# A 512-column matmul whose columns are visited in another order, in four classes of products of a hybrid decoder layer

## The chip, the cores and the metric

The kernel is written in a tile language for Trainium2 and runs on one core of one chip. The metric is device time in microseconds (us), from the launch of the program to its end. One core has five engines that run side by side: TensorE (PE in the profile, with its weight loads shown apart as PEld), VectorE (DVE), ScalarE (ACT), GpSimd (POOL) and SyncE (SP, which issues DMAs here). Each executes its own instructions in program order and waits on semaphores for the others.

## The reference

One layer of a hybrid decoder on x of shape (1, 1024, 1024): a normalised and modulated input projection, two head groups side by side (a gated linear recurrence and a chunked gated delta rule), an output projection with a residual, and a squared-ReLU MLP of width 4096. Cut to what the change touches:

```python
h = rms_norm(x, norm_mix_w[l]) * (1.0 + sc1) + sh1
proj = h @ w_in[l]
...
mix = jnp.concatenate([out_lru, out_gdn], axis=-1) @ w_out[l]
x = x + g1 * mix

h = rms_norm(x, norm_mlp_w[l]) * (1.0 + sc2) + sh2
x = x + g2 * (jnp.square(jax.nn.relu(h @ w_up[l])) @ w_down[l])

return rms_norm(x, final_norm_w)
```

## The kernel before

Every large product is made from fp32 values that have been split in two parts of fewer bits, a high part h and a low part l, in a 4-byte type (fp32r) of which the array takes one column at a time. A product is then three matmuls, h·h, h·l and l·h, all added in one PSUM tile: that is `mm3` (line 648). Its arguments are the PSUM tile p, the pair w (the stationary operand, loaded into the array) and the pair a (the moving operand, whose columns stream through the array). A matmul of the stages below has a stationary operand of 128x128 and a moving operand of 128x512, that is 512 columns of 4 bytes in each partition; its result fills a whole PSUM tile of 128x512 fp32. Column number n of the moving operand gives column number n of the result.

The stages on TensorE in order of time, with the tile names of the profile:

- the input projection (`k_p`, `z_p`, `q_p`, `v_p`, `lx_p`, `ly_p`; moving operands of 342 columns for most), with the delta rule and the recurrence worked between its products, up to 410 us;
- the output projection, `gemm_o` (line 1494), in two halves: first the delta-rule heads (`wg`), then the recurrence's (`wl`). Each half makes 8 x 2 result tiles of 4 k-steps x 3 matmuls, so 192 matmuls of 512 columns. After each `wl` row block, `norm2` (line 1523) normalises and transposes it (`h2T`);
- the MLP's first product, `up` (line 1657), from 512 to 826 us. It uses a Strassen-like scheme: for each of 16 weight blocks n, seven products numbered `at` = 1 to 7 by operand sums. `product` (line 1632) makes one, 4 k-steps x 3 matmuls = 12 matmuls of 512 columns. Number 2 is the only one that writes the PSUM tile `upy` (16 x 12 = 192 matmuls), numbers 5 and 3 write `upz` (384, half of them of number 3), numbers 1, 6, 7 and 4 write `upx` (768);
- the MLP's second product, `products` (line 1808, tile `dn`), from 826 to 1138 us, by the same scheme.

Operations are recorded first, with an estimated duration each (`length`, line 504), and then ordered by a list scheduler, which emits them from one line, so that nearly all instructions have L462 in the profile. The order of the instructions on every engine is thus set by the estimates. For a matmul of this type the estimate was taken from the size of the last dimension of the moving operand.

One other place is spoken of later: the forward substitution in `inverse` (line 1141), 31 steps on VectorE over a tile `xx` of 32 rows of 32 fp32 in each partition. Step j reads and writes n = 31 - j rows, the first m = j + 1 columns of each, so that it goes m columns in a run and then to the next row, 128 bytes further. Its products stand in `ftmp`, packed:

```python
for j in range(31):
    n, m = 31 - j, j + 1
    t3 = tmp[:, :n * m].rearrange("p (i c) -> p i c", c=m)
    V.tensor_tensor(out=t3, in0=gg[:, j + 1:, j:j + 1].to_broadcast([P, n, m]),
                    in1=xx[:, j:j + 1, 0:m].to_broadcast([P, n, m]), op=ALU.mult)
    V.tensor_tensor(out=xx[:, j + 1:, 0:m], in0=xx[:, j + 1:, 0:m], in1=t3, op=ALU.subtract)
```

Of the kernel before, what the change touches and what calls it, by code (L numbers as in the profile page):

```python
# [468 lines left out]
def free_size(ap):  # L469
    n = 1  # L470
    for d in ap.shape[1:]:
        n *= d
    return n


class Proxy:
# [27 lines left out]
    def length(self, name, out, ins, k):  # L504
        n = max([free_size(out)] + [free_size(v) for v in ins[:1]])
        ptr = sum(free_size(v) == 1 for v in ins[1:]) if n > 1 else 0
        psum = any(isinstance(v, View) and v.buf.tag == "ps" for v in ins)
        if self.eng == "PE":
            if name == "transpose":
                return 0.108  # L510
            if ins[1].dtype == F32R:
                return (max(ins[1].shape[-1], 64) / 2267.0 + 0.006) * (0.5 if ins[1].shape[0] == 64 else 1.0)
            return 4 * max(ins[1].shape[-1], free_size(ins[0])) / 2420.0 if ins[1].shape[-1] > 1 else 0.13
        if self.eng == "DVE":
            fast = name in ("tensor_scalar", "tensor_copy", "memset") and not psum
            if name == "tensor_tensor_scan":
                return 0.15 + n / 480.0
            if name == "transpose":
                return 0.05 + n / 550.0
            return (0.145 if psum else 0.155) + n / (1920.0 if fast else 960.0) + 0.06 * ptr  # L520
        if self.eng == "ACT":
            return (0.16 if psum else 0.195) + n / 1200.0 + 0.1 * max(ptr, "accum_out" in k)
        if k.get("op") == ALU.pow:
            return 0.4 + 0.156 * n
        if name == "memset":
            return 0.1 + n / 1200.0
        if name == "tensor_scalar":
            return 0.15 + n / 720.0
        if name == "scalar_tensor_tensor":
            return 0.15 + n / 380.0  # L530
        return 0.13 + n / 448.0
# [45 lines left out]
def hybrid_body(ctx, tc, x, c, norm_mix_w, norm_mlp_w, w_mod, b_mod, w_in,  # L577
# [41 lines left out]
    def ps(name):  # L619
        return buf(pp, "ps", N_PS, [P, 512], F32, name)  # L620
# [14 lines left out]
    def mm(o, lhsT, rhs, start=True, stop=True, **kw):  # L635
        PE.matmul(o, lhsT, rhs, start=start, stop=stop, **kw)
# [8 lines left out]
        rec.add("PE", several, (), {}, [x[0] for x in items], [y for x in items for y in x[1:3]], dur)  # L645
        rec.ops[-1].work = share * dur

    def mm3(p, w, a, start, stop, **kw):
        mm(p, w[0], a[0], start, False, **kw)
        mm(p, w[0], a[1], False, False, **kw)  # L650
        mm(p, w[1], a[0], False, stop, **kw)
# [167 lines left out]
    class Proj:  # L819
# [11 lines left out]
        def third(self, i):  # L831
            self.p[i] = p = ps(f"{self.name}_p{i}")
            s, _ = third(i)
            for k in range(NK):
                ks = slice(k * P, (k + 1) * P)
                mm3(p[:, 0:342], (self.w[0][:, ks], self.w[1][:, ks]), (hT[k][0][:, s], hT[k][1][:, s]),
                    k == 0, k == NK - 1)
            if i == 2:
                self.o = 3 if self.staged else 0
                self.dst = big(f"{self.name}_st", F32, T + self.o)  # L840
                if self.staged:
                    V.memset(self.dst[:, 0:3], 0.0)
                self.b = small(f"{self.name}_b", 1)
                V.tensor_copy(self.b, p[:, 340:341])
            if self.b is not None:
                for e in list(self.p):
                    _, d = third(e)
                    A.activation(self.dst[:, self.o + d.start:self.o + d.stop], self.p.pop(e)[:, 0:d.stop - d.start],
                                 AF.Identity, bias=self.b)

    class Key(Proj):
        def part(self, p, o, ks, c0, c1, start=True):
            for k in ks:
                kc = slice((k % 2) * 512 + self.h * P, (k % 2) * 512 + self.h * P + P)
                mm3(p[:, o:o + c1 - c0], (wkq[k // 2][0][:, kc], wkq[k // 2][1][:, kc]), (hT[k][0][:, c0:c1], hT[k][1][:, c0:c1]),
                    start and k == 0, k == NK - 1, skip_group_check=True)
# [147 lines left out]
    for k in range(NK):  # L1004
        a, b = (q_[:, T:T + 2] for q_ in hT[k])
# [488 lines left out]
    def gemm_o(cats, ws, t, i, name, then):  # L1494
        p = ps(name)
        s = halves[i]
        hf, tt = t // 4, t % 4
        rec.bb = True
        for k in range(4):
            ts_ = slice((k % 2) * 512 + tt * P, (k % 2) * 512 + (tt + 1) * P)  # L1500
            a, w = cats[(hf, k // 2)], ws[k]
            mm3(p, (a[0][:, ts_], a[1][:, ts_]), (w[0][:, s], w[1][:, s]), k == 0, k == 3)
        rec.bb = False
        then(p, s)

# [4 lines left out]
    for t in range(NT):  # L1510
        for i in range(2):
            gemm_o(gcat, gw_, t, i, f"wg{t}{i}",
                   lambda p, s: V.tensor_tensor(out=x1[t][:, s], in0=p, in1=x1[t][:, s], op=ALU.add))
# [68 lines left out]
    for t in range(NT):  # L1582
        for i in range(2):
            gemm_o(lcat, lw, t, i, f"wl{t}{i}",
                   lambda p, s: V.scalar_tensor_tensor(out=x1[t][:, s], in0=p, scalar=rsl[:, t:t + 1], in1=x1[t][:, s],
                                                       op0=ALU.mult, op1=ALU.add))
        if t == 0:
            dump("x1", x1[0])
        norm2(t)
# [42 lines left out]
    def product(p, at, w, start, stop):  # L1632
        rec.bb = True
        for k in range(4):
            ks, ds_ = slice(k * P, (k + 1) * P), slice((k % 2) * 512, (k % 2) * 512 + 512)
            b = opb[at][k // 2]
            mm3(p, (w[0][:, ks], w[1][:, ks]), (b[0][:, ds_], b[1][:, ds_]), start and k == 0, stop and k == 3, skip_group_check=True)
        rec.bb = False

    def relu2(dst, src_):  # L1640
# [16 lines left out]
    def up(n):  # L1657
        w = weights_up(n)
        f0, f1, ek = big(f"act{n}_0"), big(f"act{n}_1"), big(f"ek{n}")
        c11, c12, c21, c22 = f0[:, lo_], f0[:, hi_], f1[:, lo_], f1[:, hi_]  # L1660
        px, py = ps(f"upx{n}"), ps(f"upy{n}")
        product(px, 1, next(w), True, True)
        A.copy(ek[:, lo_], px)
        product(py, 2, next(w), True, True)
        V.tensor_tensor(out=c11, in0=py, in1=ek[:, lo_], op=ALU.add)
        relu2(c11, c11)
        yield
        pz = ps(f"upz{n}")
        product(px, 6, next(w), False, True)
        A.copy(ek[:, hi_], px)  # L1670
        yield
# [162 lines left out]
    for at in (1, 2, 6, 5, 7, 3, 4):  # L1834
# [18 lines left out]
        for j in range(4):  # L1853
# [10 lines left out]
            p = bank[j]  # L1864
# [49 lines left out]
```

## Time and profile before

| | |
|---|---|
| median of the runs (2) | 1149.38 us (1149.0 to 1149.75) |
| the profiled execution | 1147.2 us, of which the span of its instructions is 1145.5 us |
| TensorE busy | 1128.2 us, 98% of the span |
| VectorE, ScalarE, GpSimd busy | 833.7, 612.7, 266.0 us |
| granted TensorE clock, mean | 0.994 |
| mean DMA rate | 204 GB/s |

The page of a profile gives busy time per engine, the chain of waits that ended last, and groups of equal instructions with their count, busy time, mean duration and the idle time ahead of them. Matmuls are pipelined: a matmul of 512 columns is listed with a duration of some 395 ns, while the next one starts about 232 ns after it. What a matmul costs in a stream is therefore the step from one start to the next, which the timeline shows, and not its listed duration.

### The profile page before, as it was taken

To read this page: it belongs to the slowest core of one execution; us is meant where nothing else is said; L and a number is where in the kernel's file an instruction comes from. 1 tells how busy PE (TensorE), PEld (TensorE's weight loads), DVE (VectorE), ACT (ScalarE), POOL (GpSimd) and SP (SyncE) were. 2 spreads that over 40 slices of the span, in tenths; PEclk is the share of its full clock that TensorE was granted. 3 is DMA by queue.
4 is the path that set the end of the run, shared out by engine and by line. 5 is a ranking of instruction groups with operands and counts; after the bars stand their busy time and mean duration, and the time that the engine had idled before them with its cause. 6 is when DMAs were issued, how large, how long until landed. Compare 5 with 4: busy or idle time off the path is not lost.

```text
span 1145.5 us, 16586 instructions
## 1 busy us (share of the span) xinstructions
PE 1128.2 (98%) x6288; PEld 968.9 (85%) x6288; DVE 833.7 (73%) x1143; ACT 612.7 (53%) x961; POOL 266.0 (23%) x161
## 2 busy tenths in 40 slices
PE   8999999999999999999999999999999999999997
PEld 5889998999999987888888788887888888888886
DVE  4749998688899697879757876777775574864573
ACT  5637535445377866577554555556645433453352
POOL 1101110011112425100012231234500086823030
PEclk9999999999999999999999999999999999999999
DMA  9615834247533372331477787767999667764631
GB/s 345 215 51 205 292 111 131 92 148 235 195 114 125 105 268 94 109 135 49 156 243 247 262 277 230 246 215 253 382 392 400 238 226 272 277 231 155 220 147 74
DMA packets 126257, 233.75 MB, mean 204 GB/s; under 512 B 10785, under 2 KB 49886, under 8 KB 126178
## 3 DMA queue, kind: packets, MB, share of 16 engines
q1 hardware_dynamic: 126178, 232.71, 58.4%
q8 instruction: 49, 0.80, 0.3%
q14 instruction: 30, 0.25, 0.1%
HBM read 173.93 MB, written 58.74 MB: 203 GB/s over the span
## 4 chain that ended last, share of the span: by engine, by line
PE 85%; DVE 6%; ACT 5%; DMA 2%; issue 2%; POOL 1%; SPq 0%; POOLq 0%; ACTq 0%; DVEq 0%
PE dn L462 27%; PE upx L462 15%; PE upz L462 8%; PE k_p L462 4%; PE z_p L462 4%; PE wl L462 4%; PE upy L462 4%; PE v_p L462 4%; PE q_p L462 3%; PE ch L462 2%; PE ly_p L462 2%; PE lx_p L462 1%; ACT ta L462 1%; DVE xr L462 1%; PE cho L462 1%
## 5 line engine op out<-in xcount | busy, mean ns | idle before, releaser
L462 PE MATMUL upx<-h2h,U 128*128 128x512 f32 x512 | 168.0, 395 | 0.0
L462 PEld LDWEIGHTS upx<-h2h,U 128*128 128x128 f32 x512 | 96.0, 188 | 22.7 <-DVE U L462 0.3
L462 POOL TENSOR_TENSOR wd<-wd,wd 128x512 f32<-128x512 f32 x32 | 49.3, 1546 | 225.7 <-DMA wd<-in_w_down_dram 154.2
L462 ACT ACTIVATE act<-act 128x512 f32<-128x512 f32 x112 | 70.4, 632 | 57.0 <-DVE act L462 55.4
L462 PE MATMUL upx<-h2l,U 128*128 128x512 f32 x256 | 100.8, 394 | 0.0
L462 DVE TENSOR_TENSOR U<-wu,U 128x512 fp32r<-128x512 f32 x112 | 87.0, 795 | 18.4 <-ACT U L462 18.2
L462 PE MATMUL upz<-h2h,U 128*128 128x512 f32 x256 | 85.1, 394 | 0.0
L462 ACT CAST U<-wu 128x512 fp32r<-128x512 f32 x112 | 66.9, 618 | 32.0 <-DVE wu L462 10.4
L462 PEld LDWEIGHTS upx<-h2l,U 128*128 128x128 f32 x256 | 48.1, 188 | 11.3
L462 PEld LDWEIGHTS upz<-h2h,U 128*128 128x128 f32 x256 | 48.0, 188 | 11.3
L462 PE MATMUL upz<-h2l,U 128*128 128x512 f32 x128 | 50.5, 395 | 0.0
L462 DVE TENSOR_TENSOR act<-upz,ek 128x512 f32<-128x512 f32 x32 | 22.0, 687 | 38.9 <-PE upz L462 30.2
L462 ACT COPY ek<-upx 128x512 f32<-128x512 f32 x48 | 28.1, 585 | 37.2 <-PE upx L462 35.9
L462 PE MATMUL upy<-h2h,U 128*128 128x512 f32 x128 | 42.8, 395 | 0.2 <-DVE U L462 0.2
L462 POOL TENSOR_TENSOR xb<-xb,keep 128x512 f32<-128x512 f32 x8 | 13.5, 1697 | 117.8 <-ACT R_6h L462 82.3
L462 PE MATMUL v_p<-hl,v_wh 128*128 128x342 f32 x96 | 32.3, 337 | 2.0 <-issue 2.0
L462 DVE TENSOR_TENSOR wu<-wu,wu 128x512 f32<-128x512 f32 x48 | 33.8, 714 | 0.2
L462 PE MATMUL v_p<-hh,v_wl 128*128 128x342 f32 x96 | 32.4, 337 | 0.0
L462 PE MATMUL lx_p<-hh,lx_wh 128*128 128x342 f32 x96 | 32.2, 336 | 0.0
L462 PE MATMUL lx_p<-hl,lx_wh 128*128 128x342 f32 x96 | 32.0, 333 | 0.0
L462 PE MATMUL v_p<-hh,v_wh 128*128 128x342 f32 x96 | 31.9, 332 | 0.0
L462 PE MATMUL lx_p<-hh,lx_wl 128*128 128x342 f32 x96 | 31.7, 330 | 0.0
(587 smaller groups left out, 3580.8 us busy)
## 6 DMA issues: line engine op xcount, KB each, us to landing
L<-aod SPq DMA_DIRECT2D x56, 512.0 KB
R<-in_w_down_dram SPq DMA_DIRECT2D x40, 512.0 KB
wu<-in_w_up_dram SPq DMA_DIRECT2D x32, 512.0 KB
aod<-as SPq DMA_DIRECT2D x64, 256.0 KB
wd<-in_w_down_dram SPq DMA_DIRECT2D x32, 512.0 KB
aod<-act SPq DMA_DIRECT2D x48, 256.0 KB
sc_w<-in_w_mod_dram SPq DMA_DIRECT2D x16, 512.0 KB
x<-in_x_dram SPq DMA_DIRECT2D x16, 512.0 KB
```

What stands on the lines that cost most here:

```text
L462: op.fn(*[res(v) for v in op.a], **{n: res(v) for n, v in op.k.items()})
```

## The change

`mm3` gets an argument `walk` = (a, c). Where it is given, the moving operands and the PSUM row are both viewed as a blocks of b runs of c columns, p (a b c), and visited in the order b, a, c: c neighbouring columns from the first block, c from the second and so on through all a blocks, and then the next run of c from each. As both sides are permuted alike, column n still gives column n. With 512 columns:

| products | tile | walk (a, c) | order of columns | distance of a step to the next block |
|---|---|---|---|---|
| output projection, delta-rule half | `wg` | (2, 2) | pairs, in turn from the two halves of the row | 256 columns, 1024 bytes |
| output projection, recurrence half | `wl` | (2, 16) | runs of 16, in turn from the two halves | 256 columns, 1024 bytes |
| MLP up, number 2 | `upy` | (2, 8) | runs of 8, in turn from the two halves | 256 columns, 1024 bytes |
| MLP up, number 3 | `upz`, half of them | (16, 2) | pairs, in turn from 16 blocks | 32 columns, 128 bytes |

The estimate of a matmul's duration now takes the number of columns over all free dimensions, so that it is the same for the split view as for the plain one.

```diff
             if ins[1].dtype == F32R:
-                return (max(ins[1].shape[-1], 64) / 2267.0 + 0.006) * (0.5 if ins[1].shape[0] == 64 else 1.0)
+                return (max(free_size(ins[1]), 64) / 2267.0 + 0.006) * (0.5 if ins[1].shape[0] == 64 else 1.0)
...
-    def mm3(p, w, a, start, stop, **kw):
+    def mm3(p, w, a, start, stop, walk=None, **kw):
+        if walk:
+            pat, n = "p (a b c) -> p b a c", dict(a=walk[0], c=walk[1])
+            p, a = p.rearrange(pat, **n), [x.rearrange(pat, **n) for x in a]
         mm(p, w[0], a[0], start, False, **kw)
         mm(p, w[0], a[1], False, False, **kw)
         mm(p, w[1], a[0], False, stop, **kw)
...
-            mm3(p, (a[0][:, ts_], a[1][:, ts_]), (w[0][:, s], w[1][:, s]), k == 0, k == 3)
+            mm3(p, (a[0][:, ts_], a[1][:, ts_]), (w[0][:, s], w[1][:, s]), k == 0, k == 3, walk=(2, 2) if name[1] == "g" else (2, 16))
...
-            mm3(p, (w[0][:, ks], w[1][:, ks]), (b[0][:, ds_], b[1][:, ds_]), start and k == 0, stop and k == 3, skip_group_check=True)
+            mm3(p, (w[0][:, ks], w[1][:, ks]), (b[0][:, ds_], b[1][:, ds_]), start and k == 0, stop and k == 3, walk={2: (2, 8), 3: (16, 2)}.get(at), skip_group_check=True)
```

The order of instructions on TensorE, at the place where the output projection of the delta-rule heads begins (`wo4h` is the high part of a weight block that moves, `gch` that of the stationary operand; the last figures are the dimensions of the result), stood before so:

```order
L462 MATMUL wg_4494<-wo4l,gch_4202 128x512
L462 MATMUL wg_4494<-wo4h,gcl_4215 128x512
L462 MATMUL wg_4494<-wo5h,gch_4202 128x512
L462 MATMUL wg_4494<-wo5l,gch_4202 128x512
L462 MATMUL wg_4494<-wo5h,gcl_4215 128x512
```

and stands now so:

```order
L462 MATMUL wg_4494<-wo4l,gch_4202 128x128x2x2
L462 MATMUL wg_4494<-wo4h,gcl_4215 128x128x2x2
L462 MATMUL wg_4494<-wo5h,gch_4202 128x128x2x2
L462 MATMUL wg_4494<-wo5l,gch_4202 128x128x2x2
L462 MATMUL wg_4494<-wo5h,gcl_4215 128x128x2x2
```

No row has moved, here or elsewhere on TensorE: the rows are the same but for the split dimensions. The second place is the end of a product number 4 and the start of a number 3 in the MLP's first half (`h2h` and `h2l` are the moving operands, `U` the weights), before:

```order
L462 MATMUL upx_5354<-h2h_5613,U_4_4918 128x512
L462 MATMUL upz_5605<-h2h_5254,U_3_5628 128x512
L462 MATMUL upz_5605<-h2l_5261,U_3_5628 128x512
L462 MATMUL upz_5605<-h2h_5254,U_3_5628 128x512 x2
L462 MATMUL upz_5605<-h2l_5261,U_3_5628 128x512
```

and now:

```order
L462 MATMUL upx_5354<-h2h_5613,U_4_4918 128x512
L462 MATMUL upz_5605<-h2h_5254,U_3_5628 128x16x16x2
L462 MATMUL upz_5605<-h2l_5261,U_3_5628 128x16x16x2
L462 MATMUL upz_5605<-h2h_5254,U_3_5628 128x16x16x2 x2
L462 MATMUL upz_5605<-h2l_5261,U_3_5628 128x16x16x2
```

Here too only the dimensions differ. On VectorE, ScalarE, GpSimd and SyncE all rows stand as they stood.

## The prediction

> **What bounds the kernel now.** I read the busy times and the chain of waits on the page first, then the stages that the change touches, then the timeline of TensorE inside them. The page:
>
> ```profile
> PE 1128.2 (98%) x6288; PEld 968.9 (85%) x6288; DVE 833.7 (73%) x1143; ACT 612.7 (53%) x961; POOL 266.0 (23%) x161
> ...
> PE 85%; DVE 6%; ACT 5%; DMA 2%; issue 2%; POOL 1%; SPq 0%; POOLq 0%; ACTq 0%; DVEq 0%
> ```
>
> The first row is busy time per engine, the second the share of each in the chain that ended last. TensorE is both. The windows by stage (length, busy time of PE, PEld, DVE, ACT, POOL, granted clock, DMA share, GB/s) are `wg`, `wl` and the MLP's first half:
>
> ```profile
> 410.00:461.00 51.00, 50.35 (x223) 40.03 (x222) 43.10 (x42) 28.95 (x37) 21.58 (x9) 0.97 0.49 175
> 461.00:512.00 51.00, 51.00 (x252) 42.01 (x251) 37.77 (x86) 34.62 (x74) 4.35 (x7) 1.00 0.31 110
> 512.00:826.00 314.00, 313.82 (x1360) 253.43 (x1359) 235.01 (x312) 180.55 (x309) 70.85 (x47) 1.00 0.67 231
> ```
>
> TensorE idles 0.65 us in the first, never in the second, 0.18 us in the third. Whatever a changed matmul gains or loses, the end gains or loses. The other engines wait for TensorE, as the reader of `upz` does (count, busy, mean ns, idle before and who ended it):
>
> ```profile
> L462 DVE TENSOR_TENSOR act<-upz,ek 128x512 f32<-128x512 f32 x32 | 22.0, 687 | 38.9 <-PE upz L462 30.2
> ```
>
> So the question is the step from one matmul's start to the next in a stream of them, columns in order. Twelve matmuls of 512 columns (product number 5, tile `upz`, and the start of the one behind; start, duration):
>
> ```profile
> 697.08 0.39 PE L462 MATMUL upz<-h2h,U 128*128 128x512 f32 x1
> ...
> 699.62 0.39 PE L462 MATMUL upz<-h2h,U 128*128 128x512 f32 x1
> 699.85 0.40 PE L462 MATMUL upx<-h2h,U 128*128 128x512 f32 x1
> ```
>
> and thirteen rows of 342 columns that follow one another, the first and the last of them:
>
> ```profile
> 395.14 0.32 PE L462 MATMUL lx_p<-hl,lx_wh 128*128 128x342 f32 x1
> ...
> 397.02 0.32 PE L462 MATMUL lx_p<-hl,lx_wh 128*128 128x342 f32 x1
> ```
>
> 2.77/12 = 231 ns and 1.88/12 = 157 ns. The difference, 74 ns for 170 columns, is 0.435 ns a column, and 231 - 512 x 0.435 = 8 ns is left per matmul. A second pair of rows tells what kind of limit 0.435 is. In the `wg` stage the clock was halved for a while:
>
> ```profile
> 457.42 0.63 PE L462 MATMUL wg<-wo4h,gcl 128*128 128x512 f32 x1
> 457.85 0.63 PE L462 MATMUL wg<-wo5h,gch 128*128 128x512 f32 x1
> 458.27 0.63 PE L462 MATMUL wg<-wo5l,gch 128*128 128x512 f32 x1
> 458.70 0.63 PE L462 MATMUL wg<-wo5h,gcl 128*128 128x512 f32 x1
> ```
>
> There the step is 1.28/3 = 427 ns. Half of that is 213 ns, not 231: at the full clock a matmul takes 18 ns, 8%, more than the array's clock asks for, and at half the clock it does not. I read this as columns arriving just short of the array's full speed: a supply that is already the limit, with nothing to spare. The order of columns is what the change alters in that supply.
>
> **What the change does, part by part.** No instruction is added, removed or moved, no wait is added, and no queue is passed: on every engine the rows stand as before, with split dimensions in 768 matmuls. (That the change might not do what it says is thereby excluded: the split dimensions stand in the built program.) The estimate in `length` changes only what it gives for the split view, back to what it gave. What remains is one price per matmul for each of four walks. The 768 are 192 each, as these rows count for three of them (six groups of 16 of the 24 are shown by one each; `upz` holds numbers 5 and 3 in equal parts):
>
> ```profile
> L462 PE MATMUL wg<-wo6h,gch 128*128 128x512 f32 x16 | 6.6, 415 | 0.0
> L462 PE MATMUL wl<-wo0h,lch 128*128 128x512 f32 x16 | 6.5, 405 | 0.0
> L462 PE MATMUL upy<-h2h,U 128*128 128x512 f32 x128 | 42.8, 395 | 0.2 <-DVE U L462 0.2
> L462 PE MATMUL upy<-h2l,U 128*128 128x512 f32 x64 | 25.2, 394 | 0.0
> L462 PE MATMUL upz<-h2h,U 128*128 128x512 f32 x256 | 85.1, 394 | 0.0
> L462 PE MATMUL upz<-h2l,U 128*128 128x512 f32 x128 | 50.5, 395 | 0.0
> ```
>
> No matmul of the trace walks its columns other than in order, so the price has to be bounded by the nearest rows. These are VectorE's in the forward substitution, which reads fp32 from the same memory in short runs 128 bytes apart: singles (31 elements), pairs (60 as 30 pairs), triples (87). The groups of VectorE's instructions by form in the window of the first three steps, 135.2 to 136.8 us, and then in that of the last, 163.6 to 165.9 us, where 60 are 2 runs of 30 and 87 are 3 runs of 29:
>
> ```profile
> L462 DVE TENSOR_TENSOR xx<-xx,ftmp 128x87 f32<-128x87 f32 x1 | 0.2, 250 | 0.0
> L462 DVE TENSOR_TENSOR xx<-xx,ftmp 128x60 f32<-128x60 f32 x1 | 0.2, 221 | 0.0
> L462 DVE TENSOR_TENSOR ftmp<-gg,xx 128x60 f32<-128x60 f32 x1 | 0.2, 220 | 0.0
> L462 DVE TENSOR_TENSOR xx<-xx,ftmp 128x31 f32<-128x31 f32 x1 | 0.2, 215 | 0.0
> L462 DVE TENSOR_TENSOR ftmp<-gg,xx 128x31 f32<-128x31 f32 x1 | 0.2, 205 | 0.0
> ```
>
> ```profile
> L462 DVE TENSOR_TENSOR xx<-xx,ftmp 128x87 f32<-128x87 f32 x1 | 0.2, 250 | 0.0
> L462 DVE TENSOR_TENSOR xx<-xx,ftmp 128x60 f32<-128x60 f32 x1 | 0.2, 214 | 0.0
> ```
>
> From 60 to 87 elements it is 29 ns, 1.07 ns an element. Taken back to 31 elements that would be 221 - 31 = 190 and 220 - 31 = 189 ns; measured are 215 and 205, so a single costs 0.5 to 0.8 ns more than an element in a run: a jump takes 1.6 to 1.9 ns at least. Pairs (2.1 ns of work per jump) cost 7 ns over 30 jumps against long runs, triples nothing. So on VectorE a jump is hidden once the run behind it lasts about 2 ns.
>
> On TensorE a pair lasts 2 x 0.435 = 0.87 ns, a run of 8 lasts 3.5 ns, one of 16 lasts 7 ns. If the same floor holds for TensorE's read:
>
> - `wl` and `upy` (runs of 16 and 8): the run is longer than the floor; 0 us. The cover is the run itself; uncovered, their 32 and 64 jumps are the third rival's.
> - `wg` and `upz` number 3 (pairs): 256 jumps x 1.6 to 1.9 ns + 8 = 418 to 494 ns instead of 231, that is 187 to 263 more. Other bounds: 0 more, if a pair is what TensorE takes at once; 18 ns less, if jumping lifts the 8%. I take the middle of the floor, 225 ns, because the row at half clock says that this supply has nothing to spare. 384 x 225 = +86.4 us (71.8 to 101.0).
> - Eight of the `wg` matmuls already take 427 ns at half clock; they lose about 29 instead of 225: -1.6 us.
> - The activity that grants the clock: the halved stretch came behind 16 one-column matmuls and a gap, and cost 8 x (427 - 231) = 1.6 us. If each of the 16 starved products number 3 (12 x 456 ns = 5.5 us) brought one like it, that were up to 25 us. No row shows a TensorE that issues without a break and is starved, so I take 0 and put the 25 into the range.
>
> ```profile
> 453.28 1.95 PE L462 MATMUL lrus<-ones,msum 128*128 128x1 f32 x16 [0.43 <-POOL msum L462]
> ```
>
> Sum: 86.4 - 1.6 = +84.8 us. On the profiled execution (span 1145.5, with its ends 1147.2) that is 1232.0; the median of the runs lies 2.2 above that execution, so 1149.4 + 84.8 = 1234.
>
> The Trainium skill, "SBUF — State Buffer", Specifications, says that this memory is read in lines of 16 bytes and that a line needs at least two hits for full bandwidth. VectorE's rows agree (singles pay, pairs barely). By its letter a pair of 4-byte columns is two hits, and the sum would be +0; my floor instead counts nanoseconds per jump, and at TensorE's pace two hits last 0.87 ns. This is the first rival below.
>
> **The rivals.** *No change.* TensorE takes two neighbouring columns as one unit, and pairs are all that it needs. For it: VectorE's pairs; against it: the 8% at the full clock, which a supply with room would not show. 0 ns x 768: 1149. *Faster*, the other side: the 18 ns come from neighbouring accesses hindering one another, and taking turns between far places lifts them in all four classes: 768 x 18 = -13.8 us, 1136. It can't be over 2% (23 us), as 213 ns is the array's own pace. Against it: VectorE's jumps never gained. The point that decides is whether a walk's step falls under 231 ns.
>
> *One class of pairs alone.* With (2, 2) every second pair neighbours the last but one, and a reader that keeps both places open loses nothing; with (16, 2) a neighbour comes only after 15 others. 192 x 225 = +43.2: 1193. *Each jump costs a slot*, whatever the run: a column of the half clock, 427/512 = 0.83 ns, at 256, 256, 64 and 32 jumps: 608 x 0.83 x 192 = +97 us: 1246. Against it: VectorE's triples show no cost per jump. "PSUM — Partial Sum Buffer", Specifications, of the Trainium skill goes this way: it says that any non-contiguous pattern slows matmuls significantly, with no figure; no run here shows one yet.
>
> **The numbers.** Forecast (pairs starved, runs of 8 and 16 free) 0.44; no change 0.30; faster 0.11; one class of pairs 0.10; each jump 0.05. The time is the forecast's, 1234; its own range is 1149.4 + 71.8 - 1.6 = 1220 to 1149.4 + 101.0 - 1.6 + 25 = 1274. To hold 8 in 10 the range has to reach to no change, 1146 with the scatter of the runs, and leaves out the faster case (0.11) and the forecast's corner where both the dearest jump and the clock's whole price are paid: 1146 to 1258. 2% is about what a measurement of this kernel can tell from no change. Over 2% slower (above 1172): forecast, one class, each jump, less a hundredth for a floor that turns out small: 0.58. Within 2%: no change, nearly all of faster, and that hundredth: 0.41. Over 2% faster: 0.01.
>
> **What would show it.** In the profile after, the step between starts: about 456 ns (418 to 494) in `wg` and in `upz` of number 3, 231 in `wl` and `upy`, 231 in `upx`, `dn` and number 5. `wg` should last some 94 us instead of 51, the MLP's first half 357 instead of 314. All at 231 means no change; about 213 anywhere means the faster case; `wg` at 231 beside `upz` at 456 means one class; `upy` above `wl` above 231 means a price per jump. Steps of 427 in `upx` right behind number 3 would be the clock's price. The forecast is wrong if VectorE's floor is VectorE's own and not the memory's.

## The result and the profile after

The changed kernel takes 1209.47 us (median of 2 runs, 1208.04 to 1210.89) against 1149.38: a ratio of 1.0523, 95% interval 1.0467 to 1.0578. It is slower by 60 us. The profiled execution took 1208.04 us, its span 1206.3 us, 60.8 more than before. Of the runs reported below, one execution of the experiment with the pairs alone took 1958.33 us at a granted clock of 0.67, and is left out of every figure.

The page after, busy time per engine and the chain of waits:

```profile
PE 1190.5 (99%) x6288; PEld 973.6 (81%) x6288; DVE 831.3 (69%) x1143; ACT 612.8 (51%) x961; POOL 261.5 (22%) x161
...
PE 94%; DVE 2%; ACT 1%; issue 1%; POOL 0%; DMA 0%; POOLq 0%; SPq 0%; ACTq 0%; DVEq 0%
```

TensorE is busy for 62.3 us more with the same 6288 matmuls, its weight loads and the other engines for the same time as before within 5 us. The reader of `upz` on VectorE waits longer for TensorE, 69.9 us against 30.2 (80.1 and 38.9 with its other waits):

```profile
L462 DVE TENSOR_TENSOR act<-upz,ek 128x512 f32<-128x512 f32 x32 | 22.1, 690 | 80.1 <-PE upz L462 69.9 <-ACT ek L462 9.1 <-issue 0.9
```

So the change is in TensorE's own pace. The windows of the three changed stages, from the first matmul of each to that of the next (in the third, the last 15 us of the MLP's first half are cut off):

```profile
408.50:476.30 67.80, 67.80 (x222) 41.31 (x221) 45.75 (x42) 28.95 (x37) 20.62 (x9) 0.97 0.37 131
476.30:529.00 52.70, 52.70 (x251) 42.56 (x250) 37.65 (x84) 34.44 (x74) 4.37 (x7) 1.00 0.30 106
529.00:872.00 343.00, 343.00 (x1317) 249.11 (x1317) 224.73 (x308) 173.38 (x299) 59.81 (x40) 1.00 0.59 200
```

By the first starts in the two traces, the `wg` stage went from 50.9 to 67.8 us (+17.0), `wl` from 51.0 to 52.7 (+1.8), the MLP's first half from 314.5 to 358.1 (+43.6); the second half kept its time (319.1 both times), and what lies ahead of `wg` was 1.6 us shorter. That is the 60.8.

The 1.6 us are not the change's. In the execution profiled before, the clock was halved from 302.9 to 306.3 us, and in the one after it was not (the first row is before, the second after, PEclk the third figure from the end):

```profile
302.90:306.30 3.40, 3.40 (x15) 3.40 (x14) 1.33 (x3) 0.00 (x0) 0.00 (x0) 0.50 0.14 54
302.90:306.30 3.40, 3.40 (x26) 3.40 (x25) 2.66 (x5) 0.13 (x1) 0.00 (x0) 1.00 0.14 53
```

3.4 us at half the clock do the work of 1.7. The run with the pairs of the change alone, below, has 0.50 in this window again.

The timeline of TensorE shows the step from start to start. `wg`, pairs from two places, four steps at the end of the stage:

```profile
475.01 0.52 PE L462 MATMUL wg<-wo6h,gcl 128*128 128x512 f32 x1
475.35 0.50 PE L462 MATMUL wg<-wo7h,gch 128*128 128x512 f32 x1
475.68 0.50 PE L462 MATMUL wg<-wo7l,gch 128*128 128x512 f32 x1
476.01 0.49 PE L462 MATMUL wg<-wo7h,gcl 128*128 128x512 f32 x1
476.34 0.41 PE L462 MATMUL wl<-wo0h,lch 128*128 128x512 f32 x1
```

`wl` (runs of 16), 12 steps; `upy` (runs of 8), 12 steps; and number 3 in `upz` (pairs from 16 places), 12 steps, with two of the matmuls behind it:

```profile
522.39 0.40 PE L462 MATMUL wl<-wo0h,lch 128*128 128x512 f32 x1
...
525.29 0.41 PE L462 MATMUL wl<-wo0h,lch 128*128 128x512 f32 x1
```

```profile
708.65 0.41 PE L462 MATMUL upy<-h2h,U 128*128 128x512 f32 x1
...
711.57 0.39 PE L462 MATMUL upx<-h2h,U 128*128 128x512 f32 x1
...
714.36 0.61 PE L462 MATMUL upz<-h2h,U 128*128 128x512 f32 x1
...
719.65 0.41 PE L462 MATMUL upx<-h2h,U 128*128 128x512 f32 x1
719.89 0.39 PE L462 MATMUL upx<-h2l,U 128*128 128x512 f32 x1
```

The steps are 1.33/4 = 332, 2.90/12 = 242, 2.92/12 = 243 and 5.29/12 = 441 ns. Over all matmuls of a class the medians are 329, 242, 243 and 446; from here on, a step without a row is such a median of the differences of starts in the trace. Times 192 against 232 each, that is +18.6, +1.9, +2.1 and +41.1 us, 63.7 together. The stages grew by 62.4: in `wg`, the 0.65 us in which TensorE had idled are gone, and the eight matmuls under the half clock pay nothing, which is 0.8 us less:

```profile
472.91 0.63 PE L462 MATMUL wg<-wo5h,gch 128*128 128x512 f32 x1
473.33 0.63 PE L462 MATMUL wg<-wo5l,gch 128*128 128x512 f32 x1
473.76 0.63 PE L462 MATMUL wg<-wo5h,gcl 128*128 128x512 f32 x1
474.19 0.63 PE L462 MATMUL wg<-wo6h,gch 128*128 128x512 f32 x1
```

1.28/3 = 427 ns, as before the change: at half the clock the array is the limit and the pairs of `wg` cost nothing. What the change slows is therefore not the array but what feeds it, or what takes its results.

### The profile page after: what moved, and what is told of

It is laid out like the page before. It is cut to its first block, busy times and chain, and to the rows that moved or that the text cites. A ratio compares the mean times of both kernels' runs of the same rounds, so it can differ in the third digit from the quotient of the medians.

```text
span 1206.3 us, 16602 instructions
## 1 busy us (share of the span) xinstructions
PE 1190.5 (99%) x6288; PEld 973.6 (81%) x6288; DVE 831.3 (69%) x1143; ACT 612.8 (51%) x961; POOL 261.5 (22%) x161
## 4 chain that ended last, share of the span: by engine, by line
PE 94%; DVE 2%; ACT 1%; issue 1%; POOL 0%; DMA 0%; POOLq 0%; SPq 0%; ACTq 0%; DVEq 0%
PE dn L462 25%; PE upx L462 15%; PE upz L462 11%; PE wg L462 5%; PE upy L462 4%; PE k_p L462 4%; PE wl L462 4%; PE z_p L462 4%; PE v_p L462 4%; PE ly_p L462 3%; PE q_p L462 3%; PE lx_p L462 3%; PE ch L462 2%; PE cho L462 1%; PE sc_r L462 1%
## 5 line engine op out<-in xcount | busy, mean ns | idle before, releaser
L462 PE MATMUL upz<-h2h,U 128*128 128x512 f32 x256 | 114.2, 512 | 0.0
L462 DVE TENSOR_TENSOR U<-wu,U 128x512 fp32r<-128x512 f32 x112 | 80.5, 737 | 20.6 <-ACT U L462 19.7
L462 DVE TENSOR_TENSOR act<-upz,ek 128x512 f32<-128x512 f32 x32 | 22.1, 690 | 80.1 <-PE upz L462 69.9
L462 PE MATMUL upz<-h2l,U 128*128 128x512 f32 x128 | 65.3, 511 | 0.0
L462 PEld LDWEIGHTS upz<-h2l,U 128*128 128x128 f32 x128 | 25.0, 195 | 15.2 <-issue 11.7
```

The lines of the kernel that those rows point to most:

```text
L462: op.fn(*[res(v) for v in op.a], **{n: res(v) for n, v in op.k.items()})
```

## The experiments

The theories after the result: F, a visit to a new place in memory takes at least about 1.7 ns, unless a longer run covers it, (446 - 8)/256 = 1.71 for (16, 2); J, every jump costs a fixed slot; P, the number of places decides. And beside them: is it the moving operand's read or the PSUM write?

All experiments put other walks into single classes of products and read the step of each class from the profile. `mm3` got two more choices, the side that is permuted and the columns that are taken, and a table gives the walk of a class:

```diff
         if walk:
+            s = slice(*walk[3]) if len(walk) > 3 else slice(0, 512)
             pat, n = "p (a b c) -> p b a c", dict(a=walk[0], c=walk[1])
-            p, a = p.rearrange(pat, **n), [x.rearrange(pat, **n) for x in a]
+            side = walk[2] if len(walk) > 2 else "both"
+            p, a = p[:, s], [x[:, s] for x in a]
+            if side != "moving":
+                p = p.rearrange(pat, **n)
+            if side != "psum":
+                a = [x.rearrange(pat, **n) for x in a]
```

Tiles are renamed so that each class is one group: `mva` to `mvg` are the moving operands of the MLP's products 1 to 7, `R_1x` to `R_7x` those of its second half. In the rows below, busy divided by 192 is near the step: in the MLP's second half mostly within 2 ns, in its first half some 13 to 27 ns above it, since there each class runs in 16 separate stretches whose last matmul counts with its whole duration, and a few wait or fall under the half clock.

### Walks of many kinds

```diff
+WALKS = {"wg": (128, 2), "wl": (1, 16), ("up", 1): (16, 4), ("up", 2): (2, 4), ("up", 3): (16, 2), ("up", 4): (4, 2),
+         ("up", 5): (8, 2), ("up", 6): (64, 2), ("up", 7): (2, 2), ("dn", 1): (2, 16), ("dn", 2): (2, 8),
+         ("dn", 6): (16, 8), ("dn", 5): (16, 16), ("dn", 7): (2, 32), ("dn", 3): (2, 128)}
```

> The whole product is computed; only the walk (a, c) differs from class to class, on the moving operand and the PSUM row alike. Classes and walks: wg (128, 2); wl (1, 16), which is three dimensions without a jump; MLP up number 1 (16, 4), 2 (2, 4), 3 (16, 2), 4 (4, 2), 5 (8, 2), 6 (64, 2), 7 (2, 2); MLP down number 1 (2, 16), 2 (2, 8), 3 (2, 128), 5 (16, 16), 6 (16, 8), 7 (2, 32). Measured: the step from one matmul's start to the next; known are 232 ns in order, 446 for (16, 2), 329 for (2, 2), 242 and 243 for (2, 16) and (2, 8). Theory F, a floor of about 1.7 ns per visit of a new place, hidden by a longer run: all pairs with more than two places, (4, 2), (8, 2), (64, 2) and (128, 2), about 446 like (16, 2); runs of 4 (1.74 ns each) 232 to 245; runs of 8 and 16 at most 243. Theory J, a fixed slot per jump whatever the run, (446 - 232)/256 = 0.84 ns: (16, 4) 339, (16, 8) 285, (16, 16) 259, and (2, 32) and (2, 128) far below 242. Theory P, the number of places kept open decides: (2, 2) 329, (4, 2) between 329 and 446, rising to (16, 2), and (2, 4) much cheaper than (16, 4). The 10 ns of (2, 8) and (2, 16): if they are a price per matmul of a split pattern, (2, 32), (2, 128) and (1, 16) have them too; if they come from jumps, (2, 128) is at 232 and (1, 16) too.

The groups of TensorE by form (count, busy us, mean ns of one):

```profile
L465 PE MATMUL upz<-mve,U 128*128 128x512 f32 x192 | 96.1, 674 | 0.0
L465 PE MATMUL upx<-mvf,U 128*128 128x512 f32 x192 | 91.1, 646 | 0.0
L465 PE MATMUL upz<-mvc,U 128*128 128x512 f32 x192 | 90.2, 635 | 0.0
L465 PE MATMUL upx<-mvd,U 128*128 128x512 f32 x192 | 89.3, 630 | 0.0
L465 PE MATMUL upx<-mvg,U 128*128 128x512 f32 x192 | 65.6, 500 | 0.0
L465 PE MATMUL upy<-mvb,U 128*128 128x512 f32 x192 | 51.2, 416 | 0.0
L465 PE MATMUL upx<-mva,U 128*128 128x512 f32 x192 | 50.0, 410 | 0.0
L465 PE MATMUL dn<-R_6x,L_6x 128*128 128x512 f32 x192 | 44.6, 393 | 0.0
```

The whole kernel took 1399.79 us. Steps by walk, in ns:

| run | 2 places | 4 | 8 | 16 | 64 | 128 |
|---|---|---|---|---|---|---|
| pairs (c = 2) | 328 | 445 | 487 | 448 | 461 | 452 |
| c = 4 | 252 | | | 245 | | |
| c = 8 | 243 | | | 231 | | |
| c = 16 | 240 | | | 239 | | |
| c = 32 | 236 | | | | | |
| c = 128 | 232 | | | | | |

J falls: (16, 4) has half as many jumps as (16, 2) and would be at 339, it is at 245. F holds for pairs from 4 and more places, 1.71 to 1.87 ns a visit, though it had about 446 for all and eight places take 487; P holds for two places alone: only (2, 2) is cheaper. Runs of four columns are covered, nearly (252 is above F's 245): from two places the excess over 232 is 20, 11, 8 and 4 ns for 128, 64, 32 and 16 jumps, 0.16 to 0.25 ns a jump, and 0 for 4 jumps. So the 10 ns of `wl` and `upy` come with their jumps and not from the split form, as (2, 128) is split too. They are not a price of every jump: (16, 8) makes as many as (2, 8) and is at 231. (1, 16) was folded into a plain pattern and says nothing.

### Which side pays, and the unit

```diff
+WALKS = {"wg": (2, 16, "moving"), "wl": (2, 16, "psum"), ("up", 1): (16, 2, "moving"), ("up", 2): (16, 2, "psum"),
+         ("up", 3): (2, 2, "moving"), ("up", 4): (2, 2, "psum"), ("up", 5): (2, 8, "moving"), ("up", 6): (2, 8, "psum"),
+         ("up", 7): (128, 2, "moving"), ("dn", 1): (16, 4, "moving"), ("dn", 2): (16, 4, "psum"),
+         ("dn", 6): (15, 4, "both", (0, 480)), ("dn", 7): (15, 4, "both", (2, 482)), ("dn", 5): (128, 2, "psum"), ("dn", 3): (16, 8, "psum")}
```

> Walks on one side only: where only the moving operand is permuted, or only the PSUM row, the columns of the result land in the wrong places, so the output is not the reference's; two products of the MLP's second half are cut to 480 of 512 columns. Nothing else is left out. Moving operand alone: MLP up number 1 (16, 2), 3 (2, 2), 5 (2, 8), 7 (128, 2), wg (2, 16), MLP down 1 (16, 4). PSUM row alone: up number 2 (16, 2), 4 (2, 2), 6 (2, 8), wl (2, 16), down 2 (16, 4), 3 (16, 8), 5 (128, 2). Both sides on 480 columns with (15, 4), jumps of 32 columns: down 6 from column 0, down 7 from column 2. Theory R, the read of the moving operand pays: moving alone gives the steps known from both sides, 446, 329 and 243, PSUM alone stays at 232. Theory W, the PSUM write pays: the other way round. Mixed: (16, 2) from one side and (2, 2) from the other. For the cut products: in order they would take 8 + 480 x 0.435 = 217 ns. If the unit that is visited is an aligned group of four columns, the product that starts at column 2 splits every run over two units and takes 240 x 1.71 + 8 = 418, against 217 to 230 for the one that starts at column 0; if the unit is the run itself, both are alike.

Moving operand alone (16, 2) and (2, 2), PSUM row alone (16, 2) and (2, 2), and then the two cut products, from column 2 and from column 0:

```profile
L465 PE MATMUL upx<-mva,U 128*128 128x512 f32 x192 | 90.3, 634 | 0.0
L465 PE MATMUL upz<-mvc,U 128*128 128x512 f32 x192 | 66.8, 504 | 0.0
L465 PE MATMUL upy<-mvb,U 128*128 128x512 f32 x192 | 47.7, 396 | 0.0
L465 PE MATMUL upx<-mvd,U 128*128 128x512 f32 x192 | 47.3, 394 | 0.0
...
L465 PE MATMUL dn<-R_7x,L_7x 128*128 128x480 f32 x192 | 79.6, 593 | 0.0
L465 PE MATMUL dn<-R_6x,L_6x 128*128 128x480 f32 x192 | 44.1, 393 | 0.0
```

With the moving operand alone the steps are 450, 330 and 243 for (16, 2), (2, 2) and (2, 8), as with both sides; with the PSUM row alone every walk, pairs too, is at 231 to 233. The read of the moving operand pays for everything. And the unit of that read is an aligned group of four columns, 16 bytes: runs of four from column 0 take 229 ns for 480 columns, the same runs two columns later 407. That is near the 418 that F gives if each run falls on two units.

### Why two places are cheaper

```diff
+            if side == "half":
+                p = p[:, 0:256]
+                a = [x.rearrange("p (a b u c) -> p b a u c", u=2, **n)[:, :, :, 0, :] for x in a]
...
+WALKS = {("up", 6): (2, 2, "moving", (0, 256)), ("up", 7): (2, 2, "half"), ("up", 4): (2, 2, "moving", (0, 128)),
+         ("up", 3): (3, 2, "moving", (0, 480)), ("dn", 6): (2, 2, "moving", (0, 480)), ("dn", 7): (16, 2, "half"), ("dn", 3): (4, 2, "moving", (0, 256))}
```

> Why (2, 2) is cheaper than the other pairs, 329 against 445 to 487. The moving operand alone is walked, in seven classes, and each matmul of them covers only part of its 512 columns; the result is written in order. So the output is not the reference's and the work is less. Unit: an aligned group of four columns, 16 bytes. MLP up 6: (2, 2) on 256 columns, halves 128 columns apart. Up 4: (2, 2) on 128 columns, 64 apart. Up 3: (3, 2) on 480 columns, three places 160 apart. Up 7: two places 256 apart, but only the first pair of every unit is read, 256 columns, so that no unit is visited twice. MLP down 6: (2, 2) on 480 columns, 240 apart. Down 7: 16 places, only the first pair of every unit, 256 columns. Down 3: (4, 2) on 256 columns, four places 64 apart. Theory K, the read keeps the last two units open and a second visit of one of them costs (329 - 8)/128 - 1.71 = 0.80 ns: up 6 8 + 128 x 1.25 = 168, down 6 308, up 4 88 if nothing else limits a matmul so short; all the others pay 1.71 per visit: up 3 8 + 240 x 1.71 = 418, up 7 227, down 7 227, down 3 227. Theory D, two far places alternating is cheap in itself, by their distance: up 7 168 like a (2, 2) of 256 columns, and up 6, with another distance, not 168 but up to 227.

(3, 2) on 480 columns; (2, 2) on 480; two places without a second visit; 16 places without a second visit; (4, 2) on 256 columns:

```profile
L465 PE MATMUL upz<-mvc,U 128*128 128x480 f32 x192 | 73.1, 545 | 7.4 <-ACT U L465 7.4
L465 PE MATMUL dn<-R_6x,L_6x 128*128 128x480 f32 x192 | 59.2, 478 | 0.0
L465 PE MATMUL upx<-mvg,U 128*128 128x256 f32 x192 | 49.6, 429 | 0.0
...
L465 PE MATMUL dn<-R_7x,L_7x 128*128 128x256 f32 x192 | 43.9, 406 | 0.0
L465 PE MATMUL dn<-R_3x,L_3x 128*128 128x256 f32 x192 | 43.9, 404 | 1.7 <-DVE L_3x L465 1.7
```

Steps: (2, 2) on 256 columns 166 (K 168) and on 480 columns 307 (K 308), whatever the distance of the places, 128, 240 or 256 columns. Two places with one visit per unit 244, 16 places 228, (4, 2) 225 (K 227 each): no discount without a second visit soon. So it is the second visit that is cheap, not the alternation, and D falls. K's limit of two units falls too: three places take 354, (354 - 8)/240 = 1.44 ns a visit, between 1.25 for two and 1.71 for four, where K said 1.71. The discount shrinks with the number of other units in between and is gone at three; how the read does that isn't shown. The matmul of 128 columns took 111 instead of 88; what limits it there isn't shown.

### The two halves of the change apart

Runs alone (`wl`, number 2), and pairs alone (`wg`, number 3):

```diff
+WALKS = {"wl": (2, 16), ("up", 2): (2, 8)}
```

> The change without its pairs: wl walks (2, 16) and MLP up number 2 walks (2, 8), as in the changed kernel; wg and number 3 go in order. By the steps of the profile after, 192 x (242 - 232) + 192 x (243 - 232) = 4.0 us, so 1149.4 + 4.0 = 1153.4, a ratio of 1.0035. The prediction on record had 0 for these two classes: a ratio of 1.000. If the remaining 60 us came from pairs and runs together (through the clock or waits), it would be well above 1.0035.

Measured: 1152.84 against 1147.02 us, a ratio of 1.0050, interval 1.0035 to 1.0065. It is small but not zero; the expected 1.0035 is its lower end. In its profile the `wl` stage grew by 1.8 and the MLP's first half by 2.2 us, together the expected 4.0.

```diff
+WALKS = {"wg": (2, 2), ("up", 3): (16, 2)}
```

> The change without its runs of 16 and 8: wg walks (2, 2) and MLP up number 3 walks (16, 2); wl and number 2 go in order. By the steps of the profile after: 192 x (329 - 232) + 192 x (446 - 232) = 59.7 us less 0.8 for the eight matmuls that the halved clock held at 427 before and holds at 426 after; so about +59 us, 1206 from 1147, a ratio of 1.051. If the parts only add up, the changed kernel's 60.1 is this and the 4 us of the runs, less some 3 of scatter; the prediction on record had 84.8 for this part, a ratio of 1.074.

Measured: 1206.52 us (median of three, 1205.24 to 1208.31) against 1146.89, a ratio of 1.0516, interval 1.0484 to 1.0548, as the steps say. The parts add up to the change's 1.0523 within these intervals.

### Does any order beat the plain one?

```diff
+WALKS = {"wg": (32, 8), "wl": (64, 8), ("up", 1): (4, 8), ("up", 2): (8, 8), ("up", 3): (8, 16), ("up", 4): (4, 16),
+         ("up", 5): (4, 32), ("up", 6): (8, 32), ("up", 7): (2, 64), ("dn", 1): (4, 4), ("dn", 2): (8, 4),
+         ("dn", 6): (32, 4), ("dn", 5): (64, 4), ("dn", 7): (8, 8), ("dn", 3): (16, 8)}
```

> The whole product, all walks on both sides, all runs of whole units of four columns: does any order beat the 232 ns of the plain one? wg (32, 8), wl (64, 8); MLP up 1 (4, 8), 2 (8, 8), 3 (8, 16), 4 (4, 16), 5 (4, 32), 6 (8, 32), 7 (2, 64); MLP down 1 (4, 4), 2 (8, 4), 6 (32, 4), 5 (64, 4), 7 (8, 8), 3 (16, 8). The theory of a floor per visit gives 232 to 252 for all: every unit is visited once and fully used, as in order. The rival that was called faster in the prediction, accesses of neighbours hindering one another, gives under 226 for some of them, down to 213.

(8, 4), (4, 4), (64, 4) and (32, 4):

```profile
L465 PE MATMUL dn<-R_2x,L_2x 128*128 128x512 f32 x192 | 53.5, 444 | 0.0
L465 PE MATMUL dn<-R_1x,L_1x 128*128 128x512 f32 x192 | 51.6, 435 | 0.0
...
L465 PE MATMUL dn<-R_5x,L_5x 128*128 128x512 f32 x192 | 44.8, 395 | 0.0
...
L465 PE MATMUL dn<-R_6x,L_6x 128*128 128x512 f32 x192 | 43.5, 386 | 0.0
```

Whole units in another order are not all alike: 278 and 268 ns for jumps of 64 and 128 columns, 233 for jumps of 8, and 225 for (32, 4), jumps of 16 columns. The last is under the 232 of the plain order. The rest of the table lies at 232 to 249; (64, 8) in `wl` is the plain order by another name. Neither expectation had 268 or 278, and one walk met the rival's. The whole kernel took 1175.54 us. So that walk went into all matmuls of 512 columns in the output projection and the MLP:

```diff
+WALKS = {"wg": (32, 4), "wl": (32, 4), **{(s, i): (32, 4) for s in ("up", "dn") for i in range(1, 8)}}
```

> The whole product, in the order that was the only one under 232 ns in a single class, (32, 4), runs of one unit with jumps of 16 columns: 226 ns in number 6 of the MLP's second half. Here it is the walk of all matmuls of 512 columns in both halves of the output projection and of the MLP, 192 + 192 + 1344 + 1320 = 3048. Theory S, the gain belongs to the order of the units: 3048 x 6 = 18 us less, 1147 to 1129, a ratio of 0.984. Theory C, 226 was particular to that class (its tiles' addresses, its neighbours): the steps scatter around 232 and the ratio is 0.995 to 1.005.

It takes 1129.8 us (1129.52 to 1133.73) against 1147.86, a ratio of 0.985, interval 0.9826 to 0.9874: 18 us faster than the kernel before, as theory S had it, and some 80 faster than the changed one. Its page and its largest group, whose mean was 395:

```profile
PE 1109.5 (98%) x6288; PEld 966.6 (86%) x6288; DVE 831.3 (74%) x1143; ACT 613.1 (54%) x961; POOL 267.6 (24%) x161
...
L465 PE MATMUL upx<-h2h,U 128*128 128x512 f32 x512 | 164.7, 388 | 0.0
```

All classes have medians of 224 to 227 ns. Which side, and which jumps:

```diff
+WALKS = {"wg": (32, 4), "wl": (32, 4), ("up", 1): (32, 4, "moving"), ("up", 2): (32, 4, "psum"), ("up", 5): (64, 4, "moving"),
+         ("up", 6): (40, 4, "moving", (0, 480)), ("up", 7): (24, 4, "moving", (0, 480)), ("up", 4): (20, 4, "moving", (0, 480)),
+         ("up", 3): (16, 4, "moving", (0, 448)), ("dn", 1): (32, 4), ("dn", 2): (32, 8), ("dn", 6): (1, 480, "moving", (0, 480)),
+         ("dn", 5): (32, 4, "moving"), ("dn", 7): (10, 4, "moving", (0, 480)), ("dn", 3): (30, 4, "moving", (0, 480))}
```

> Which side and which jump. Moving operand alone, PSUM row alone or parts of the columns, so the output is not the reference's, and the products named with 480 or 448 columns do that much less. (32, 4): both sides in wg, wl and MLP down 1; moving alone in up 1 and down 5; PSUM alone in up 2. Moving alone: up 5 (64, 4); on 480 columns up 6 (40, 4), up 7 (24, 4), up 4 (20, 4), down 7 (10, 4), down 3 (30, 4), that is jumps of 12, 20, 24, 48 and 16 columns; on 448 columns up 3 (16, 4), jumps of 28; down 2 (32, 8) on both sides; down 6 in order on 480 columns, as the measure. In order 480 columns take 8 + 480 x 0.435 = 217 and 448 take 203. Theory S: (32, 4) 226 wherever the moving operand walks it, 232 with PSUM alone; the other jumps then show for which distances between units the read gains (under 217, under 203) or loses. Theory C: (32, 4) at 232 in the other classes.

Jumps of 24 columns on 480; (32, 4) with PSUM alone; (32, 4) with the moving operand alone; 480 columns in order:

```profile
L465 PE MATMUL upx<-mvd,U 128*128 128x480 f32 x192 | 57.8, 458 | 0.0
...
L465 PE MATMUL upy<-mvb,U 128*128 128x512 f32 x192 | 47.5, 395 | 0.0
...
L465 PE MATMUL dn<-R_5x,L_5x 128*128 128x512 f32 x192 | 43.4, 386 | 0.0
...
L465 PE MATMUL dn<-R_6x,L_6x 128*128 128x480 f32 x192 | 42.0, 380 | 0.0
```

The moving operand alone gives the whole gain (225), PSUM alone none (232). On 480 columns, where in order is 218, jumps of 12 columns take 214, 16 take 215, 48 take 216, 20 take 240 and 24 take 287; on 448 columns jumps of 28 take 205 against a calculated 203. The order in which whole units follow one another thus matters in both directions. By which rule was not settled: the distance of the jump and the number of places changed together in these walks.

## Why the prediction came out as it did

- **What bounds the kernel**: right. TensorE's step is the time; the rest of the program did not move but for the clock's 1.6 us, and the sum of four classes times 192 gives the 60.8 us within 3.
- **The supply has nothing to spare**: right. At the full clock pairs cost 97 and 214 ns; at half the clock, in the rows above, those of `wg` cost nothing. Of the 18 ns that the plain order takes above the array's 213, some 7 belong to that order, as (32, 4) shows.
- **Number 3, pairs from 16 places**: right in mechanism and size. The floor of 1.6 to 1.9 ns per jump was read from VectorE; 456 forecast, 446 measured: 192 x 10 = 1.9 us less than forecast. TensorE's read has a floor of this size, 1.71 ns here. That it is the same one is not shown, as no run changes VectorE's walk; the close agreement may in part be luck.
- **`wg`, pairs from two places**: this is the term that was mis-sized. The step "if the same floor holds" took one price for both classes; (2, 2) pays 1.25 ns per jump, 329 instead of 456, 192 x 127 = 24.4 us less. The rival that kept neighbouring places open pointed the right way and was itself too strong: it had 0 for `wg`, and the second visit of a unit is cheaper, not free.
- **Runs of 16 and 8**: forecast 0, measured 10 and 11 ns, 4.0 us together. The cover by the run is not complete: between the two halves of the row 0.16 to 0.25 ns per jump is left, for other whole units nothing (231 ns for (16, 8)) or much more (278 ns for (8, 4)).
- **The activity behind the clock**: 0 was right. The `upx` matmuls right behind number 3 start 0.24 us apart (719.65 and 719.89), and from the start of `wl` on the clock stays at 1.00 in the windows above; it was halved in the `wg` stage, as before. The eight matmuls there were to lose 29 ns each and lost nothing, since 329 lies under their 427. The 94 us named as a sign for `wg` left out the forecast's own 1.6 for them.
- Together, with the measured steps, the forecast's 86.4 becomes 86.4 - 24.4 - 1.9 + 4.0 = 64.1 us. Less 0.8 for the eight matmuls and 0.65 for the idle time that went, it is 62.6, against the 62.4 by which the stages grew; less the clock's 1.6 us ahead of `wg`, 61.0 against 60.8. The time lies inside the range, which reached down to no change, so that this says little; it is below the forecast's own 1220 because of `wg` alone.
- **No change** fell, and with it the rule of two hits taken by its letter: "SBUF — State Buffer", Specifications, of the Trainium skill asks for at least two hits on a line of 16 bytes. The line of 16 bytes is what the shifted run shows (229 against 407). But a pair is two hits, and pairs from 16 places cost 446 instead of 232. For this read, four columns of 4 bytes on a line are needed, as the floor in nanoseconds had it.
- **Each jump a slot** fell by (16, 4), 245 and not 339. The sentence of the Trainium skill, "PSUM — Partial Sum Buffer", Specifications, that any non-contiguous pattern slows matmuls significantly, isn't borne out for the row of results here: pairs from 2, 16 and 128 places in PSUM alone stay at 232 or 233.
- **Faster** fell for the four walks of the change, but not as such: the order (32, 4) of the moving operand takes 225 ns, and all matmuls together give 18 us. Whether it is because neighbouring accesses hinder one another less isn't shown. The objection, that VectorE's jumps never gained, proved nothing for TensorE.

## What to carry to other kernels

The matmuls of this kernel, with 512 columns of 4 bytes in 232 ns, run close to the limit of their moving operand's read, so the order of its columns is a cost to be looked at: keep every visit to a whole aligned group of four columns, which is worth nearly a factor of two here, and don't split it. The order in which such groups follow one another gave from 3% less (225 ns) to 20% more (278 ns), with 480 columns up to 32% more (287 against 218), and is found by trying: the step from start to start, class by class, tells a dozen orders apart in one profiled run. The order of columns in PSUM was free in every walk tried, none of them with runs under two columns.

## What was not expected of the hardware

A second visit to a 16-byte group soon after the first is cheaper, but not free: per pair 1.25 ns with two places in turn, 1.44 with three, 1.71 with four. And plain order is not the best one: with jumps of 16 columns between whole groups 512 columns take 225 ns instead of 232, with jumps of 64 columns 278. Both are open in their cause.
